# Gate products of a two-layer trunk: branch loads a group ahead, operand splits spread, last token sums in four steps

## The chip, the cores and the metric

The kernel runs on one core of a Trainium2 chip. The metric is the device time of one execution in microseconds (us), as the median of several runs.

## The reference

The model is a trunk of two layers over 1024 latent tokens and 256 context tokens with 1024 channels. In each layer an input projection feeds four token mixers (a, b, cc, d), each of 256 channels, and 4 x 1024 gate columns. The part that matters here is the merge:

```python
def merge_branches(a, b, cc, d, zg, w_a, w_b, w_c, w_d, w_o):
    ga, gb, gc, gd = jnp.split(jax.nn.sigmoid(zg), N_BRANCH, axis=-1)
    m = ga * (a @ w_a) + gb * (b @ w_b) + gc * (cc @ w_c) + gd * (d @ w_d)
    return m @ w_o
```

Here zg is `h @ w_in` for the gate columns, with h the modulated and normed tokens. All data are 32-bit floats. In the last layer only the 1024 latent tokens go through the merge.

## The kernel before

**Precision.** A product of two float arrays is made from three matmuls (`mm3`, L432 to L434). Each operand is split into a high part, rounded on ACT by a copy (L427), and a low part, the difference, on DVE (L428). The matmuls are high by high, high by low, low by high. `split` issues the two instructions of one operand.

**The stage.** `gates_last` (L1210) makes the merge of the last layer. It works through 16 groups: four blocks d of 256 output channels, and for each the four branches i. A group needs the gate (1024 input channels by 256 columns, for 1024 tokens), which goes into two PSUM tiles A of 128x1024, and the branch product (256 channels by 256 columns), which goes into tiles X and T. DVE multiplies the two and adds the product to the sum m.

**Seven products.** Groups 0 and 1 make the gate from four blocks of the weights (x11, x12, x21, x22), 24 matmuls each. From group 2 on, the gate is a 2x2 block matrix product with seven block products instead of eight, of 12 matmuls each. They use sums of weight blocks (s1, s2, s3, s4, made on POOL in `begin`, L1283, and `s4`, L1287) and sums of token blocks (T1 to T4). The list `plan` (L1353) gives the order x11, s2, x12, x22, s3, s1, s4, the quarter q of A that each fills, and its token block. After x11 ACT copies the quarter out (L1360); after s2 DVE makes u2 (L1362); after x12 DVE makes c11 (L1365) and ACT its sigmoid; after s3 c21 (L1368); after s1 three more sums (L1370 to L1372) and a sigmoid (L1373); after s4 the last sum (L1375) and its sigmoid.

**Token sums.** T1, T2 and T3 are made in groups 0 and 1 by the generator `sides` (L1226): four steps, each with three sums on DVE (L1233), three differences on POOL (L1236) and their splits. It is advanced three times after each half product. T4 (L1240 to L1249) takes the room of token block 12 and can only be made after group 1. Group 2 makes all of its four steps at once, by `self.finish(side)` ahead of its first product.

**Order of the work.** Each engine runs its instructions in the order in which the program issues them. The list `ops` holds the splits of the weight operands of all groups in their order of use; `ready(n + 3)` issues them up to two ahead of the product that comes next. The gate weights come through three buffers (`graw`) on the SP queue; a load waits until the last reader of its buffer is done.

**Branches.** `bh_load` (L1323) loads the two halves of the group's branch from DRAM by the POOL queue (L1327), through one buffer `br`, splits each half into bh and bl, and splits the branch weights into wbh and wbl. It is issued after x12 in groups 0 and 1, and after s2 from group 2 on. In the group's last part 24 matmuls form the branch product (tiles X and T, L1390), and DVE multiplies and adds (L1393 to L1396).

Of the kernel before, what the change touches and what calls it, by code (L numbers as in the profile page):

```python
# [8 lines left out]
F32 = mybir.dt.float32  # L9
F32R = mybir.dt.float32r  # L10
BF16 = mybir.dt.bfloat16
I32 = mybir.dt.int32
AF = mybir.ActivationFunctionType
# [404 lines left out]
class Trunk:  # L418
# [791 lines left out]
    def gates_last(self, p, mp):  # L1210
# [9 lines left out]
        Y = {}  # L1220
# [5 lines left out]
        def sides():  # L1226

            for k in range(4):
                t = [mp.tile([128, 1024], F32, name="mr", bufs=2) for _ in range(2)]
                y11, y12, y22 = t[0][:, :512], t[0][:, 512:], t[1][:, :512]  # L1230
                for y, n in ((y11, "11"), (y12, "12"), (y22, "22")):
                    h, lo = Y[n][k]
                    nc.vector.tensor_tensor(y, h.bitcast(F32), lo.bitcast(F32), op=OP.add)  # L1233
                    yield 1
                for o, x, y, n in ((y11, y12, y11, "T1"), (y12, y22, y12, "T3"), (y22, y22, y11, "T2")):
                    nc.gpsimd.tensor_tensor(o, x, y, op=OP.subtract)  # L1236
                    yield 1
                    self.split(*Y[n][k], o)

            while "T4" not in Y:  # L1240
                yield 2
            for k in range(4):
                t = mp.tile([128, 1024], F32, name="mr", bufs=2)
                y21, t2 = t[:, :512], t[:, 512:]
                for y, n in ((y21, "21"), (t2, "T2")):
                    h, lo = Y[n][k]
                    nc.vector.tensor_tensor(y, h.bitcast(F32), lo.bitcast(F32), op=OP.add)
                nc.gpsimd.tensor_tensor(y21, y21, t2, op=OP.subtract)
                self.split(*Y["T4"][k], y21)  # L1249
                yield 3  # L1250

        side = sides()
        ops = []
# [7 lines left out]
        def product(o, w, y, start, stop):  # L1261
            for k in range(4):
                self.mm3(o, w[0][:, k, :], w[1][:, k, :], *Y[y][k], start=start and k == 0, stop=stop and k == 3)
# [3 lines left out]
        def make(gi):  # L1267

            d, i = groups[gi]
            S = {"d": d, "i": i}  # L1270
            G.append(S)

            def x(j, b):
                return S["raw"][j][:, 4 * b:4 * b + 4, :]

            def begin():
                S["raw"] = [st.get()[0] for _ in range(2)]
                S["wb"] = st.get()[0]
                if gi >= 2:
                    s1, s2, s3 = ([p.tile([128, 4, 128], F32, name=n) for n in ("s1", "s2", "s3")])  # L1280
                    for o, a, b, op in ((s1, x(1, 0), x(1, 1), OP.add), (s2, s1, x(0, 0), OP.subtract),
                                        (s3, x(0, 0), x(1, 0), OP.subtract)):
                        nc.gpsimd.tensor_tensor(o, a, b, op=op)  # L1283
                    S["s"] = s1, s2, s3

            def s4():
                nc.gpsimd.tensor_tensor(S["s"][1], x(0, 1), S["s"][1], op=OP.subtract)  # L1287

            if gi < 2:
                names = [("x11", lambda: x(0, 0)), ("x12", lambda: x(0, 1)), ("x21", lambda: x(1, 0)), ("x22", lambda: x(1, 1))]  # L1290
            else:
                names = [("x11", lambda: x(0, 0)), ("s2", lambda: S["s"][1]), ("x12", lambda: x(0, 1)), ("x22", lambda: x(1, 1)),
                         ("s3", lambda: S["s"][2]), ("s1", lambda: S["s"][0]), ("s4", lambda: S["s"][1])]
            for n, f in names:
                def prep(n=n, f=f):
                    if n == "x11":
                        begin()
                    S[n] = operand(f())
                    if n == "s2":
                        S["late"] = True  # L1300
                    if n == "x12" and S.pop("late", None):
                        s4()
                ops.append(prep)
# [5 lines left out]
        def ready(n):  # L1309
            while done[0] < min(n, len(ops)):  # L1310
                ops[done[0]]()
                done[0] += 1
        n = 0
        ready(2)
        add, AC = OP.add, nc.scalar.activation
        halves = [slice(0, 512), slice(512, 1024)]
        for gi, (d, i) in enumerate(groups):
# [2 lines left out]
            q = [A[j // 2][:, halves[j % 2]] for j in range(4)]  # L1320
            g = [p.tile([128, 1024], F32, name="g", bufs=2) for _ in range(2)]

            def bh_load():  # L1323
                S["b"] = []
                for k in range(2):
                    b = p.tile([128, 1024], F32, name="br", bufs=1)
                    nc.gpsimd.dma_start(b, self.br[i][k * 128:(k + 1) * 128, :1024])  # L1327
                    bh, bl = p.tile([128, 1024], F32R, name=f"bh{k}"), p.tile([128, 1024], F32R, name=f"bl{k}")
                    S["b"].append((b, bh, bl))
                    self.split(bh, bl, b)  # L1330
                wh, wl = p.tile([128, 2, 256], F32R, name="wbh"), p.tile([128, 2, 256], F32R, name="wbl")
                self.split(wh, wl, S["wb"])
                S["w"] = wh, wl

            if gi < 2:
                for j, w in enumerate(("x11", "x12", "x21", "x22")):
                    ready(n + 3)
                    for t in range(2):
                        product(q[j // 2 * 2 + t], S[w], "12"[j % 2] + "12"[t], j % 2 == 0, j % 2 == 1)
                        for _ in range(3):  # L1340
                            next(side)
                    n += 1
                    if j == 1:
                        bh_load()
                    if j % 2:
                        AC(g[j // 2], A[j // 2], AF.Sigmoid)
            else:
                if gi == 2:
                    Y["T4"] = Y["12"]
                    self.finish(side)  # L1350
                u2 = p.tile([128, 512], F32, name="u2")
                c11, c12, c21, c22 = g[0][:, :512], g[0][:, 512:], g[1][:, :512], g[1][:, 512:]
                plan = [("x11", 0, "11"), ("s2", 1, "T2"), ("x12", 0, "21"), ("x22", 2, "T4"), ("s3", 1, "T3"),  # L1353
                        ("s1", 3, "T1"), ("s4", 0, "22")]
                for j, (w, o, y) in enumerate(plan):
                    ready(n + 3)
                    product(q[o], S[w], y, True, True)
                    n += 1
                    if w == "x11":
                        AC(c11, q[0], AF.Copy)  # L1360
                    elif w == "s2":
                        nc.vector.tensor_tensor(u2, q[1], c11, op=add)  # L1362
                        bh_load()
                    elif w == "x12":
                        nc.vector.tensor_tensor(c11, q[0], c11, op=add)  # L1365
                        AC(c11, c11, AF.Sigmoid)
                    elif w == "s3":
                        nc.vector.tensor_tensor(c21, q[1], u2, op=add)  # L1368
                    elif w == "s1":
                        nc.vector.tensor_tensor(c22, q[3], c21, op=add)  # L1370
                        nc.vector.tensor_tensor(c12, q[3], u2, op=add)
                        nc.vector.tensor_tensor(c21, q[2], c21, op=add)  # L1372
                        AC(g[1], g[1], AF.Sigmoid)  # L1373
                    elif w == "s4":
                        nc.vector.tensor_tensor(c12, q[0], c12, op=add)  # L1375
                        AC(c12, c12, AF.Sigmoid)
# [3 lines left out]
            if i == 0:  # L1380
                self.mp = m = mp.tile([128, 2, 1024], F32, name="mp")
            wh, wl = S["w"]
            for j in range(2):
                ready(n + 2 + j)
                for t in range(2):
                    s = halves[t]
                    o = self.ps.tile([128, 512], F32, name="XT"[t])
                    for k in range(2):
                        c = slice(128 * j, 128 * j + 128)
                        self.mm3(o, wh[:, k, c], wl[:, k, c], S["b"][k][1][:, s], S["b"][k][2][:, s],  # L1390
                                 start=(k == 0), stop=(k == 1))
                    if i == 0:
                        nc.vector.tensor_tensor(m[:, j, s], o, g[j][:, s], op=OP.mult)  # L1393
                    else:
                        nc.vector.tensor_tensor(g[j][:, s], o, g[j][:, s], op=OP.mult)
                        nc.vector.tensor_tensor(m[:, j, s], m[:, j, s], g[j][:, s], op=add)  # L1396
# [778 lines left out]
```

## Time and profile before

| | |
|---|---|
| median of 3 runs | 3649.33 us (3646.88 to 3649.39) |
| profiled execution: time | 3648.42 us |
| profiled execution: span | 3646.6 us |
| mean granted TensorE clock | 0.964 |
| PE busy | 3376.2 us, 93% |
| DVE busy | 2287.4 us, 63% |
| ACT busy | 1616.0 us, 44% |
| POOL busy | 928.9 us, 25% |

The page of the profile belongs to one execution. PE is TensorE's matmuls, PEld its weight loads, DVE VectorE, ACT ScalarE, POOL GpSimd, SP the engine that issues most DMAs. A busy PE is not PE at its peak: a matmul at a lower granted clock is busy for longer. "Idle before" is the time an engine waited ahead of an instruction, with what ended that wait. L427 is line 427 of the kernel.

### The profile page before, as it was taken

How to read it: one execution, taken by the hardware profiler on the slowest of the kernel's cores; microseconds unless marked ns; L12 is line 12 of the kernel's file. 1: busy time of each engine (PE TensorE's matmuls, PEld its weight loads, DVE VectorE, ACT ScalarE, POOL GpSimd, SP SyncE). 2: the span in 40 equal slices, each digit the busy share in tenths (PEclk: the TensorE clock that was granted, in tenths of full speed). 3: DMA queues.
4: the chain of work that ended last, by engine and by line, in shares of the span. 5: the costliest groups of instructions: out<-in, count | busy, mean ns of one | idle time of the engine just before them, and what ended most of it. 6: DMA issues, size and time to landing. Idle time of an engine off the chain costs nothing. (4 is left out here: it accounts for less than half of the span.)

```text
span 3646.6 us, 47270 instructions
## 1 busy us (share of the span) xinstructions
PE 3376.2 (93%) x18567; PEld 2590.7 (71%) x18567; DVE 2287.4 (63%) x3116; ACT 1616.0 (44%) x2203; POOL 928.9 (25%) x798
## 2 busy tenths in 40 slices
PE   7999999999998899999998999878888896999997
PEld 5996788888875566666665797656666675888885
DVE  5856512223265677777776784654555457999997
ACT  4125411111144566556664423532222254777776
POOL 3105100000025433333221112422122143535430
PEclk9999999999999899999999999989999897999998
DMA  6113233333045788888888313222222368999995
GB/s 207 36 54 98 78 98 99 103 93 107 25 168 199 260 293 288 286 287 288 283 288 283 95 41 98 59 65 80 90 76 78 125 218 306 385 387 378 390 385 199
DMA packets 300177, 672.45 MB, mean 184 GB/s; under 512 B 32991, under 2 KB 138325, under 8 KB 299954
## 3 DMA queue, kind: packets, MB, share of 16 engines
q1 hardware_dynamic: 267410, 554.50, 42.7%
q0 software_dynamic: 32368, 114.85, 10.4%
q8 instruction: 146, 2.39, 0.3%
q14 instruction: 77, 0.63, 0.1%
q10 hardware_dynamic: 176, 0.08, 0.0%
HBM read 610.33 MB, written 54.84 MB: 182 GB/s over the span
## 5 line engine op out<-in xcount | busy, mean ns | idle before, releaser
L428 DVE TENSOR_TENSOR wlo<-wraw,whi 128x1024 fp32r<-128x1024 f32 (+1 forms) x882 | 1023.6, 1205 | 470.1 <-ACT whi L427 465.1
L427 ACT ACTIVATE whi<-wraw 128x1024 fp32r<-128x1024 f32 (+1 forms) x882 | 862.4, 1027 | 292.9 <-PE A L434 264.5
L432 PE MATMUL A<-hTh,whi 128*128 128x512 f32 x1056 | 426.0, 403 | 11.3 <-DVE u L1362 11.0
L432 PE MATMUL A<-whi,xh 128*128 128x512 f32 x1024 | 418.2, 408 | 1.4 <-ACT whi L427 1.4
L434 PE MATMUL A<-hTh,wlo 128*128 128x512 f32 x1056 | 412.9, 391 | 3.6 <-DVE wlo L428 3.6
L433 PE MATMUL A<-hTl,whi 128*128 128x512 f32 x1056 | 412.6, 391 | 3.8 <-POOL hTl L684 2.1
L433 PE MATMUL A<-wlo,xh 128*128 128x512 f32 x1024 | 404.3, 395 | 2.0 <-DVE wlo L428 1.1
L434 PE MATMUL A<-whi,xl 128*128 128x512 f32 x1024 | 402.4, 393 | 0.5 <-DVE xl L428 0.5
L1963 POOL TENSOR_SCALAR oh<-cs,slot 128x128 bf16<-128x128 f32 x232 | 278.2, 1216 | 1.0
L2071 POOL DMA_INDIRECT x<-y,idx x31 | 50.6, 1631 | 843.2 <-DVE y L2070 843.2
L432 PEld LDWEIGHTS A<-hTh,whi 128*128 128x128 f32 x1056 | 199.1, 189 | 67.9 <-DVE u L1362 17.2
L432 PEld LDWEIGHTS A<-whi,xh 128*128 128x128 f32 x1024 | 193.8, 189 | 66.4 <-issue 15.1
L434 PEld LDWEIGHTS A<-hTh,wlo 128*128 128x128 f32 x1056 | 198.4, 188 | 48.3 <-DVE wlo L428 5.7
L433 PEld LDWEIGHTS A<-hTl,whi 128*128 128x128 f32 x1056 | 199.1, 189 | 44.1 <-POOL hTl L684 3.0
L433 PEld LDWEIGHTS A<-wlo,xh 128*128 128x128 f32 x1024 | 194.0, 189 | 45.5 <-DVE wlo L428 10.2
L434 PEld LDWEIGHTS A<-whi,xl 128*128 128x128 f32 x1024 | 193.4, 189 | 43.3 <-DVE xl L428 1.2
L1173 ACT ACTIVATE g<-A 128x1024 f32<-128x1024 f32 x32 | 32.9, 1029 | 398.8 <-PE A L434 325.6
L432 PE MATMUL A<-whi,gh 128*128 128x512 f32 x512 | 208.5, 407 | 0.2 <-ACT gh L427 0.2
L433 PE MATMUL A<-wlo,gh 128*128 128x512 f32 x512 | 202.5, 396 | 0.9 <-DVE wlo L428 0.9
L434 PE MATMUL A<-whi,gl 128*128 128x512 f32 x512 | 201.6, 394 | 0.0
L948 DVE SCALAR_TENSOR_TENSOR cacc<-cy,par,cacc 128x1310 f32<-128x1310 f32 (+1 forms) x120 | 190.9, 1591 | 3.4
L433 PE MATMUL A<-wlo,hTh 128*128 128x256 f32 x592 | 168.8, 285 | 10.1 <-DVE wlo L428 10.1
(469 smaller groups left out, 6542.7 us busy)
## 6 DMA issues: line engine op xcount, KB each, us to landing
wraw<-in_w_up_e_dram SPq DMA_DIRECT2D x126, 1024.0 KB, 6.7
wraw<-in_w_gate_e_dram SPq DMA_DIRECT2D x125, 1024.0 KB, 8.4
wraw<-in_w_down_e_dram SPq DMA_DIRECT2D x122, 1024.0 KB, 7.6
wraw<-in_w_in_dram SPq DMA_DIRECT2D x96, 512.0 KB, 4.2
wraw<-in_w_mod_dram SPq DMA_DIRECT2D x68, 512.0 KB, 4.3
br<-br POOLq DMA_DIRECT2D x32, 512.0 KB, 3.7
wraw<-in_w_mod_dram SPq DMA_DIRECT2D x14, 1024.0 KB, 8.3
h<-h POOLq DMA_DIRECT2D x16, 520.0 KB, 3.2
```

Of the source, the lines that this page charges most:

```text
L427: nc.scalar.activation(hi, src, AF.Copy)
L428: (eng or nc.vector).tensor_tensor(lo, src, hi.bitcast(F32), op=OP.subtract)
L432: mm(out, lh, rh, start=start, stop=False)
L433: mm(out, lh, rl, start=False, stop=False)
L434: mm(out, ll, rh, start=False, stop=stop)
L948: nc.vector.scalar_tensor_tensor(acc[:, j, :], y[:, w:w + n_out], wc, acc[:, j, :], op0=OP.mult, op1=OP.add)
L1173: nc.scalar.activation(g[:, :SEQ], A, AF.Sigmoid)
L1963: eng.tensor_scalar(S["oh"][:, t, :], iota, self.slot[:, t, e:e + 1], None, op0=OP.is_equal)
L2071: nc.gpsimd.indirect_dma_start(out=self.x1[l][:, :], out_offset=bass.IndirectOffsetOnAxis(ap=S["idx"][:, :1], axis=0), in_=y, in_offset=No ...
```

## The change

The branches of a group are loaded a group ahead, on ACT's queue, into two buffers: the first group's ahead of the loop, and each next group's just before the branch products. `bh_load` is cut into three parts, `branch(0)`, `branch(1)` (a half of the branch each) and `branch(2)` (the branch weights). They are issued after x12, x21 and x22 in groups 0 and 1, and after s2, x12 and x22 from group 2 on. The T4 steps of group 2 are issued one ahead of each product, each step's split one step later. Group 2 alone makes x22, which needs T4, as its last product, and the sum and the sigmoid that need it (`sum21`) after it.

```diff
             while "T4" not in Y:
                 yield 2
+            last = None
             for k in range(4):
...
                 nc.gpsimd.tensor_tensor(y21, y21, t2, op=OP.subtract)
-                self.split(*Y["T4"][k], y21)
+                if last:
+                    self.split(*last)
+                last = (*Y["T4"][k], y21)
                 yield 3
+            self.split(*last)
+            yield 3
...
+            if gi == 2:
+
+                names.append(names.pop(3))
             for n, f in names:
...
         n = 0
+        B = {}
+
+        def b_load(gi):
+            i = groups[gi][1]
+            B[gi] = [p.tile([128, 1024], F32, name="br", bufs=2) for _ in range(2)]
+            for k in range(2):
+                nc.scalar.dma_start(B[gi][k], self.br[i][k * 128:(k + 1) * 128, :1024])
         ready(2)
+        b_load(0)
...
-            def bh_load():
-                S["b"] = []
-                for k in range(2):
-                    b = p.tile([128, 1024], F32, name="br", bufs=1)
-                    nc.gpsimd.dma_start(b, self.br[i][k * 128:(k + 1) * 128, :1024])
-                    bh, bl = p.tile([128, 1024], F32R, name=f"bh{k}"), p.tile([128, 1024], F32R, name=f"bl{k}")
-                    S["b"].append((b, bh, bl))
-                    self.split(bh, bl, b)
-                wh, wl = p.tile([128, 2, 256], F32R, name="wbh"), p.tile([128, 2, 256], F32R, name="wbl")
-                self.split(wh, wl, S["wb"])
-                S["w"] = wh, wl
+            S["b"] = []
+
+            def branch(k):
+
+                if k == 2:
+                    wh, wl = p.tile([128, 2, 256], F32R, name="wbh"), p.tile([128, 2, 256], F32R, name="wbl")
+                    self.split(wh, wl, S["wb"])
+                    S["w"] = wh, wl
+                    return
+                bh, bl = p.tile([128, 1024], F32R, name=f"bh{k}"), p.tile([128, 1024], F32R, name=f"bl{k}")
+                self.split(bh, bl, B[gi][k])
+                S["b"].append((None, bh, bl))
 
             if gi < 2:
...
-                    if j == 1:
-                        bh_load()
+                    if j:
+                        branch(j - 1)
                     if j % 2:
                         AC(g[j // 2], A[j // 2], AF.Sigmoid)
             else:
                 if gi == 2:
                     Y["T4"] = Y["12"]
-                    self.finish(side)
...
+                if gi == 2:
+                    plan.append(plan.pop(3))
+
+                def sum21():
+                    nc.vector.tensor_tensor(c21, q[2], c21, op=add)
+                    AC(g[1], g[1], AF.Sigmoid)
                 for j, (w, o, y) in enumerate(plan):
                     ready(n + 3)
+                    if gi == 2:
+                        next(side, None)
                     product(q[o], S[w], y, True, True)
                     n += 1
                     if w == "x11":
                         AC(c11, q[0], AF.Copy)
                     elif w == "s2":
                         nc.vector.tensor_tensor(u2, q[1], c11, op=add)
-                        bh_load()
+                        branch(0)
                     elif w == "x12":
                         nc.vector.tensor_tensor(c11, q[0], c11, op=add)
                         AC(c11, c11, AF.Sigmoid)
+                        branch(1)
+                    elif w == "x22":
+                        branch(2)
+                        if gi == 2:
+                            sum21()
                     elif w == "s3":
                         nc.vector.tensor_tensor(c21, q[1], u2, op=add)
                     elif w == "s1":
                         nc.vector.tensor_tensor(c22, q[3], c21, op=add)
                         nc.vector.tensor_tensor(c12, q[3], u2, op=add)
-                        nc.vector.tensor_tensor(c21, q[2], c21, op=add)
-                        AC(g[1], g[1], AF.Sigmoid)
+                        if gi > 2:
+                            sum21()
...
             wh, wl = S["w"]
+            if gi + 1 < len(groups):
+                b_load(gi + 1)
             for j in range(2):
                 ready(n + 2 + j)
```

## Rows read from the trace of the kernel before

**Rows 1.** Windows: groups 0 and 1, group 2, groups 3 to 15, and their sum.

```profile
core 0: us, PE busy (x) PEld busy (x) DVE busy (x) ACT busy (x) POOL busy (x), PEclk, DMA share, GB/s
2343.69:2409.70 66.01, 57.89 (x241) 45.76 (x241) 40.05 (x51) 22.39 (x33) 25.84 (x21) 0.95 0.26 80
2409.70:2458.82 49.12, 29.43 (x110) 22.79 (x109) 25.26 (x37) 11.60 (x18) 12.07 (x11) 0.79 0.18 54
2458.82:2888.15 429.33, 355.21 (x1407) 278.99 (x1406) 221.36 (x314) 116.91 (x179) 83.44 (x80) 0.92 0.27 84
sum 544.46, PE 442.53 PEld 347.53 DVE 286.68 ACT 150.90 POOL 121.35; mean PE 147.51 PEld 115.84 DVE 95.56 ACT 50.30 POOL 40.45
```

**Rows 2.** Waits of PE in the stage: us in total, times, longest.

```profile
PE A L432 <- DVE g L1365: 58.5, 14, 6.9
PE A L432 <- ACT g L1360: 24.4, 14, 15.4
PE A L432 <- DVE u L1362: 11.0, 14, 0.8
```

**Rows 3.** Timeline of PE, group 3: start us, us, instruction, idle before.

```profile
2458.82 0.39 PE L432 MATMUL A<-hTh,whi 128*128 128x512 f32 x1
...
2462.39 0.50 PE L432 MATMUL A<-T2h,whi 128*128 128x512 f32 x1 [0.69 <-ACT g L1360]
...
2466.19 0.50 PE L432 MATMUL A<-hTh,whi 128*128 128x512 f32 x1 [0.78 <-DVE u L1362]
...
2475.24 0.77 PE L432 MATMUL A<-T3h,whi 128*128 128x512 f32 x1 [3.29 <-DVE g L1365]
...
2479.52 0.39 PE L432 MATMUL A<-T1h,whi 128*128 128x512 f32 x1
...
2490.40 0.39 PE L432 MATMUL A<-hTh,whi 128*128 128x512 f32 x1
```

**Rows 4.** Windows, group 3: x12 and x22, then s3; columns as rows 1.

```profile
2466.20:2471.60 5.40, 5.40 (x24) 4.41 (x24) 1.06 (x1) 0.63 (x1) 0.54 (x1) 1.00 0.38 125
...
2475.20:2479.60 4.40, 4.37 (x13) 3.51 (x14) 1.29 (x2) 2.12 (x4) 2.44 (x2) 0.64 0.15 50
```

**Rows 5.** Timelines of DVE, POOL and ACT, group 3: the chain to L1365.

```profile
2465.44 0.69 DVE L1362 TENSOR_TENSOR u<-A,g 128x512 f32<-128x512 f32 x1 [1.86 <-PE A L434]
...
2467.57 0.54 POOL L1327 DMA_DIRECT2D br<-br  x1 [10.61 <-DMA wraw<-in_w_in_dram]
...
2470.97 1.06 ACT L427 ACTIVATE bh<-br 128x1024 fp32r<-128x1024 f32 x1 [7.17 <-DMA br<-br]
...
2474.41 0.68 DVE L1365 TENSOR_TENSOR g<-A,g 128x512 f32<-128x512 f32 x1
```

**Rows 6.** Groups of instructions by form, in the stage: busy us, mean ns, idle before.

```profile
L427 ACT ACTIVATE bh<-br 128x1024 fp32r<-128x1024 f32 x32 | 33.8, 1056 | 134.1 <-DMA br<-br 134.1
L428 DVE TENSOR_TENSOR bl<-br,bh 128x1024 fp32r<-128x1024 f32 x32 | 39.2, 1225 | 95.5 <-ACT bh L427 95.4
L427 ACT ACTIVATE whi<-s 128x512 fp32r<-128x512 f32 x56 | 33.1, 614 | 0.0
L1373 ACT ACTIVATE g<-g 128x1024 f32<-128x1024 f32 x14 | 14.9, 1061 | 105.6 <-DVE g L1372 105.6
L1283 POOL TENSOR_TENSOR s<-wraw 128x512 f32<-128x512 f32 x28 | 41.3, 1476 | 121.0 <-DVE wlo L428 119.1 <-DMA wraw<-in_w_in_dram 1.9
```

**Rows 7.** From issue to landing in the stage: branch loads (L1327), then weight loads (L135).

```profile
DMA to landing us min/median/max: 3.3/3.7/5.8
...
DMA to landing us min/median/max: 2.7/3.8/6.0
```

**Rows 8.** Timeline of PE, group 2: the first matmul of s2.

```profile
2427.98 0.79 PE L432 MATMUL A<-T2h,whi 128*128 128x512 f32 x1 [15.40 <-ACT g L1360]
```

**Rows 9.** Timelines of PE, POOL and ACT, group 0.

```profile
2372.11 0.79 PE L432 MATMUL X<-bh,wbh 128*128 128x512 f32 x1 [5.37 <-ACT wbh L427]
...
2355.45 4.64 POOL L1236 TENSOR_TENSOR mr<-mr 128x512 f32<-128x512 f32 x3 [3.13 <-DVE mr L1233]
...
2372.07 1.28 ACT L1346 ACT_TABLE_LOAD   x1
```

## The prediction

> **What bounds the kernel now.** I first cut the stage out of the trace by windows [rows 1]: its 16 groups take 544.5 us of the span, 66.0 for groups 0 and 1, 49.1 for group 2 and 429.3 for groups 3 to 15, which is 33.0 each. PE is busy 442.5 of the 544.5, but that busy time includes matmuls at half clock: the granted clock is 0.92 in the last stretch and 0.79 in group 2. So the question is what PE does between and during its waits. The waits of PE [rows 2] name one big one: the third quarter of a group waits for the DVE add of L1365, 58.5 us in 14 waits. Two small ones, on L1360 and L1362, stand beside it.
>
> The matmuls of group 3 in order of time [rows 3] give the price. x11 starts at 2458.82, s2 at 2462.39, x12 at 2466.19, s3 at 2475.24, s1 at 2479.52, and the next group at 2490.40. The last part holds 48 matmuls (s1, s4 and the branch products) in 10.88 us without a break, so one matmul of 128x512 costs 0.2267 us. x12 and x22, 24 matmuls, need 5.44 and are done at 2471.63: s3 then waits 3.6 us, and its 12 matmuls take 4.28 instead of 2.72. That is the clock: the granted clock is 1.00 while x12 and x22 run and 0.64 in s3 [rows 4], so part of s3 runs at 1.2 GHz where the others have 2.4. One wait costs 3.6 + 1.6 = 5.2 us here, and 33.0 - 26.4 = 6.6 on average over the groups, since a late branch transfer lengthens it.
>
> What is L1365 late for? Nothing of its own; x12 was done at 2469. It is queued on DVE behind the second branch's split. The chain [rows 5]: u at 2465.44 on DVE, then the first branch's bl, which frees the one buffer; POOL issues the second load at 2467.57, ACT splits it at 2470.97, then DVE does bl, wbl, the split of s3, and L1365 at 2474.41. s3 starts 0.15 us after that add ends. PE waits for it although s3 writes the other half of the PSUM tile; the same is seen at s2 (for L1360) and x12 (for L1362), so a product waits for all earlier readers of its tile A.
>
> **The change in a steady group (3 to 15).** I set time 0 at x11's first matmul and lay the new order out, with the durations of [rows 6]: 1.06 for bh, 1.23 for bl, 0.61 for a whi or wbh, 1.06 for a sigmoid of 1024 columns; 0.7 for a DVE operation of 512 columns by L1365 [rows 5].
> PE keeps its two small waits: s2 at 3.57, x12 at 7.37, x22 at 10.09, end of x22 at 12.81.
> ACT: copy of c11 until 3.5, whi of x22, then bh0 at once, because both branches were loaded a group ahead, until 5.1, whi of s3 until 5.7. DVE: u at 6.6 to 7.3, bl0 to 8.5, wlo of s3 to 9.1, then L1365, waiting for x12, 10.3 to 11.0. So s3, due at 12.81, finds operand and PSUM tile ready 1.8 us early: the wait goes, and with it the low clock.
> Next on ACT: sigmoid of c11 to 11.65, bh1 to 12.7, whi of s1, wbh, whi of s4 to 14.3. On DVE: bl1 to 14.0, wlo of s1 to 14.6, wbl, wlo of s4 to 15.9. s1 starts at 15.53 and its first low-part weights are wanted 0.45 later: 1.4 us of margin, the least of the group. s4 at 18.25 and the branch products at 20.97 find theirs. What stalls would be late next is thus s1's operand.
> POOL loses 32 issues of 0.54 (first: L1327 in [rows 5]); it was not on the path except through the buffer. It does the next group's sums at 14.6 to 19, before they are wanted at 21.
> The 32 loads go to ACT's queue, after the sigmoid of c12 at 23.9. No row of this stage has an ACT issue; the nearest is POOL's 0.54. I take that, 1.1 a group: ACT has only one whi (0.6) before the next copy of c11 at 29.3, so 4.8 us are free and the cost is nothing. The bounds are 0 and, if ACT were held until the data land, the 5.8 of the slowest landing; that case is a rival below. The loads land 3.3 to 5.8 after issue [rows 7], at 31 at the latest, that is 4.4 in the next group, and bh0 could begin as late as 9 before L1365 passes 12.8. Two buffers are free by then: bl1 ended at 14.
> The group is 3.57 + 3.80 + 5.44 + 2.72 + 10.88 = 26.4 us. 13 groups of 33.0 become 13 of 26.4: **-86**.
>
> **Group 2.** In the kernel before all four T4 steps run before s2: PE waits 15.40 us [rows 8] and starts again at half clock. After the change one step is issued ahead of each of the first four products, the last split ahead of the fifth, and T4's product is last. Laid out in the same way: DVE has two more adds and a split per step, so u is at 6.7, L1365 ends at 11.75, and s3, now straight behind x12 (done at 10.1), waits 1.6; s4 waits 0.6 for L1368. x22 runs from 20.6 to 23.3. A new wait follows. x22's split is now late (to 18.4), and it is the last reader of a weight buffer that the next group's second load waits for. That load takes 3.8 [rows 7]: 22.4. POOL then needs two sums of 1.48 [rows 6], ACT 0.6 for whi of the next s2, and only behind that stands wbh, 26.6. The branch products start 3.3 late, with 1.6 of low clock as in s3: the group ends at 33.8. It was 49.1: **-15**. Bounds: 29 (no wait at all) to 39 (landing at 6.0 and lower clock longer).
>
> **Groups 0 and 1.** Here the change moves a split to the wrong side. wbh was issued after x12; PE still waited 5.37 for it, at 2372.11 [rows 9], because of the one buffer. Now branch(2) is issued after x22, behind the third and fourth steps of the T sums, whose chain is serial: two adds (1.4), 4.64 on POOL [rows 9], split and its DVE half (1.3). The second step's POOL work ends at 2360.1. Behind it ACT now does bh0, the table load of 1.28 [rows 9], a sigmoid, a whi and the split, so DVE ends that step at 2364.3; the third step ends with bh1, a whi and bl1 among it at 2373.3; the fourth reaches its T3 split on ACT at 2378.3, and wbh ends at 2378.9. PE waits 6.9 longer, and about 0.9 more in low clock and for wbl. Groups 0 and 1 lost 66.0 - 240 x 0.2267 = 11.6 in all; 6.2 of that is other small waits, and I take 2.6 of it as gained in group 1, where no T step stands among the branch splits any more. Net **+5**, bounds -5 and +12.
>
> **The sum.** -86 - 15 + 5 = -96. The profiled execution took 3648.4; that gives 3552. The median of the three runs stands 0.9 above it: **3553**. The work behind the stage starts on the last branch product, so the gain should pass to the end whole.
>
> **The rivals.**
> *The clock swings all the same.* Two short waits remain in every group (0.69 and 0.78, [rows 3]). If the clock fell after them as it does after s3's wait, each group would give 1.6 back, 13 x 1.6 = 21: 3574. Against it: after both of them x12 and x22 run at 1.00 [rows 4].
> The Trainium skill, page "TensorE: Matmul & The Clock Gate", section "A second HAM failure mode: psum-queue depth-cycling", holds that frequent micro-idles between groups of matmuls are enough to make the clock swing. By that rule this rival would be the likely case; the trace of this kernel does not agree at these two waits.
> *s1 waits in s3's place.* Its operand stands behind bh1 and bl1 with 1.4 us to spare. If DVE and ACT run 3.4 late (sums on POOL slow DVE, a branch lands late), PE waits 2 us a group, 26 in all: 3579.
> *The loads come no earlier.* If the loads on ACT were held until the group they belong to, L1365 would stay late in groups 3 to 15 and only -15 + 5 would remain: 3643. For it: nothing but that ACT is in order; against it, both buffers are free 10 us before.
> *Slower: ACT held by its loads.* If an issue on ACT holds the engine for h until its data land, the next copy of c11, and so s2, is late by 2h - 4.8, and 1.6 of low clock follows. At 3.7 [rows 7] that is 4.2 a group, 55 in all: 3608. It decides against the change from h = 5.3 on, where 13 x 7.4 eats the 96; at 5.8 it is 13 x 8.4 = 109: 3662. Against it: POOL's issues took 0.54 whatever the landing.
>
> **How the numbers follow.** Forecast 0.75, s1 waits 0.08, clock 0.07, loads no earlier 0.03, ACT held 0.04, and 0.03 for something in the code around (other buffer addresses at the start of the stage) that I cannot see. The forecast's own bounds are 3553 - 15 (groups 0 to 2 at their good ends) and, with s1 or the clock, 3579; a little beyond gives 3538 to 3582. A measurement of this kernel can tell some 0.2% from no change, 7 us. "Loads no earlier" lies inside that and counts as same, with a part of the unseen; half of "ACT held" is slower. Faster 0.93; same 0.04; slower 0.03.
>
> **What would show it.** Right: no PE wait on L1365 worth naming in groups 3 to 15, s3 at clock 1.00, groups 26 to 27 us long, ACT idle before bh gone, group 0's wait on wbh longer than 5.4 (about 12), and a wait of 3 to 4 ahead of group 2's branch products. Wrong: groups of 28 or more with a wait ahead of s1 or s2, an ACT issue of microseconds, or a granted clock below 1.00 in groups that have only the two small waits.

## The result and the profile after

The changed kernel takes 3552.78 us (median of 6 runs, 3550.01 to 3554.93) against 3649.95 us (6 runs, 3646.88 to 3654.79): a ratio of 0.9732, 95% interval 0.9719 to 0.9744. The forecast was 3553.

The windows of the same three stretches, in the profile of the changed kernel, answer to [rows 1]:

```profile
2340.31:2410.95 70.64, 57.67 (x241) 46.48 (x241) 39.93 (x51) 22.17 (x33) 23.97 (x17) 0.90 0.27 88
2410.95:2445.65 34.70, 27.83 (x109) 20.77 (x108) 26.07 (x38) 11.51 (x18) 11.56 (x8) 0.95 0.22 68
2445.65:2791.32 345.67, 326.53 (x1408) 261.68 (x1407) 234.57 (x313) 116.55 (x179) 75.40 (x55) 1.00 0.32 102
```

Groups 0 and 1 are 4.6 us longer, group 2 is 14.4 shorter, groups 3 to 15 are 83.7 shorter: together the stage loses 93.4 of its 544.5. The granted clock of the last stretch rose from 0.92 to 1.00. The waits of PE in the stage answer to [rows 2]:

```profile
PE X L432 <- ACT wbh L427: 14.4, 2, 11.8
PE A L432 <- DVE u L1386: 11.3, 14, 1.2
PE A L432 <- ACT g L1384: 9.6, 14, 0.7
...
PE A L432 <- DVE g L1389: 1.7, 1, 1.7
```

L1389 is the c11 add, L1365 before: its 58.5 us in 14 waits are one wait of 1.7, in group 2. The two small waits per group are unchanged (L1384 and L1386, before L1360 and L1362), except that L1384 lost the 15.4 us of group 2. The largest are now two waits for wbh: that of group 0, 5.37 before [rows 9] and 11.8 now, and a new one in group 2. The matmuls of group 3 in order of time, for [rows 3]:

```profile
2445.65 0.39 PE L432 MATMUL A<-hTh,whi 128*128 128x512 f32 x1
...
2449.22 0.50 PE L432 MATMUL A<-T2h,whi 128*128 128x512 f32 x1 [0.69 <-ACT g L1384]
...
2453.03 0.50 PE L432 MATMUL A<-hTh,whi 128*128 128x512 f32 x1 [0.79 <-DVE u L1386]
...
2458.64 0.39 PE L432 MATMUL A<-T3h,whi 128*128 128x512 f32 x1
...
2472.24 0.39 PE L432 MATMUL A<-hTh,whi 128*128 128x512 f32 x1
```

s3 starts without a wait, and the group takes 26.6 us. DVE and ACT of the same group show why, against [rows 5]:

```profile
2452.28 0.69 DVE L1386 TENSOR_TENSOR u<-A,g 128x512 f32<-128x512 f32 x1 [1.87 <-PE A L434]
2452.89 1.22 DVE L428 TENSOR_TENSOR bl<-br,bh 128x1024 fp32r<-128x1024 f32 x1
2454.02 0.69 DVE L428 TENSOR_TENSOR wlo<-s,whi 128x512 fp32r<-128x512 f32 x1
2456.12 0.69 DVE L1389 TENSOR_TENSOR g<-A,g 128x512 f32<-128x512 f32 x1 [1.42 <-PE A L434]
2458.46 1.23 DVE L428 TENSOR_TENSOR bl<-br,bh 128x1024 fp32r<-128x1024 f32 x1 [1.65 <-ACT bh L427]
...
2469.32 0.63 ACT L1405 ACTIVATE g<-g 128x512 f32<-128x512 f32 x1 [1.36 <-DVE g L1404]
2469.33 0.81 ACTq L1328 DMA_DIRECT2D br<-br  x2
2470.24 0.63 ACT L427 ACTIVATE whi<-wraw 128x512 fp32r<-128x512 f32 x1 [0.29 <-ACT g L1405]
```

The add now waits for PE, not PE for the add: it starts 10.5 us into the group (the forecast said 10.3) and ends 1.8 ahead of s3. The second half's split comes behind it. The two loads of the next group take 0.81 us of ACT's queue. They are issued while the sigmoid ahead of them still runs, so ACT itself is idle for only 0.29 us before its next copy.

### The profile page after: what moved, and what is told of

Read it like the earlier page. It is cut to its first block, busy times and chain, and to the rows that moved or that the text cites. A ratio compares the mean times of both kernels' runs of the same rounds, so it can differ in the third digit from the quotient of the medians.

```text
span 3548.2 us, 47246 instructions
## 1 busy us (share of the span) xinstructions
PE 3340.8 (94%) x18567; PEld 2570.2 (72%) x18567; DVE 2300.6 (65%) x3116; ACT 1614.9 (46%) x2203; POOL 921.2 (26%) x766
## 3 DMA queue, kind: packets, MB, share of 16 engines
q1 hardware_dynamic: 267410, 554.50, 43.9%
## 4 chain that ended last, share of the span: by engine, by line
PE 49%; issue 7%; DVE 7%; DMA 3%; ACT 3%; POOL 1%; SPq 0%; POOLq 0%; ACTq 0%; DVEq 0%
PE A L432 13%; PE A L433 13%; PE A L434 12%; PE X L1983 4%; DVE wlo L428 2%; DMA x<-y,idx 1%; PE T L2086 1%; ACT whi L427 1%; DVE cacc L948 1%; PE T L2039 1%; DVE y L2101 1%; PE X L434 0%; PE X L433 0%; PE X L432 0%; POOL oh L1994 0%
```

## The experiments

Each variant starts from the changed kernel. The table gives the time of the stage from the profile of each, cut as in [rows 1], since code outside it is the same. The ratio is to the kernel before, measured beside it.

| kernel | groups 0, 1 | group 2 | groups 3 to 15 | stage | median | ratio, 95% interval |
|---|---|---|---|---|---|---|
| before | 66.0 | 49.1 | 429.3 | 544.5 | 3649.95 | |
| changed | 70.6 | 34.7 | 345.7 | 451.0 | 3552.78 | 0.9732 (0.9719 to 0.9744) |
| POOL's queue | 71.2 | 34.9 | 345.6 | 451.7 | 3558.33 | 0.9749 (0.9732 to 0.9765) |
| one buffer, splits spread | 79.1 | 43.9 | 359.6 | 482.7 | 3587.81 | 0.9833 (0.9816 to 0.9849) |
| loads ahead, splits together | 55.5 | 33.4 | 345.7 | 434.6 | 3537.60 | 0.9692 (0.9676 to 0.9708) |
| T4 steps at once | 71.0 | 39.2 | 345.6 | 455.8 | 3560.46 | 0.9752 (0.9736 to 0.9769) |
| other quarters | 71.0 | 33.5 | 318.5 | 422.9 | 3525.01 | 0.9656 (0.9637 to 0.9674) |
| branch splits early | 55.5 | 32.6 | 345.7 | 433.9 | 3534.82 | 0.9680 (0.9658 to 0.9702) |
| early, other quarters | 55.5 | 31.7 | 318.5 | 405.7 | 3507.93 | 0.9605 (0.9589 to 0.9621) |
| sixteen issues | 81.4 | 39.0 | 391.8 | 512.1 | 3615.05 | 0.9900 (0.9883 to 0.9916) |

**Does the queue matter?**

```diff
-                nc.scalar.dma_start(B[gi][k], self.br[i][k * 128:(k + 1) * 128, :1024])
+                nc.gpsimd.dma_start(B[gi][k], self.br[i][k * 128:(k + 1) * 128, :1024])
```

> The changed kernel with its 32 branch loads on POOL's queue again, still a group ahead and into two buffers. Theory (the gain is the removed wait of s3; which queue issues the loads does not matter): 3553, within 0.2%; groups 3 to 15 stay at 26.6 us each, POOL gets 32 issues of about 0.54 us back and no PE wait changes. Rival (the queue is part of the gain, because POOL's loads stand behind its stores and sums): the groups after a store (each fourth) lose several us again, in all 10 to 30 us.

The steady groups are the same within a few hundredths, but the median was 5.5 us above that of the changed kernel, measured on another occasion. So both were run again, side by side.

> The changed kernel as it is, beside its variant with the loads on POOL's queue, on the same chip. The variant's first run gave 3558.3 with the same 26.6 us groups; its excess over 3552.8 lay outside the stage. Theory (which queue issues the loads does not matter, the excess was the chip or the executions): the two ratios come out within 0.1% of each other. Rival (POOL's issues cost something outside the stage's PE row): the variant is 4 to 6 us longer here too.

> The loads on POOL's queue again, for the comparison with the changed kernel on the same chip. Theory: equal within 4 us. Rival: longer by 4 to 6 us, outside the groups 3 to 15.

The changed kernel gave 3553.12 (ratio 0.9725, 0.9712 to 0.9738), the variant 3554.76 (0.9732, 0.9719 to 0.9746), in 5 runs each, and the stage 451.7 and 450.2 in their profiles. The queue does not matter to the time within this noise: the medians are 1.6 us apart. The medians from issue to landing do differ; the two lines are POOL's in the first of its runs, then ACT's in the changed kernel:

```profile
DMA to landing us min/median/max: 3.7/4.5/6.5
```

```profile
DMA to landing us min/median/max: 3.4/3.7/5.8
```

The 0.8 us are not like for like. The loads go out in pairs, and the trace has a landing for all 32 of POOL's loads but for only 20 of ACT's. The first of a pair lands after 3.85 us on POOL and 3.48 on ACT (medians), the second after 4.55 and 4.59. Either way the data are there long before the next group wants them. The Trainium skill says in "DMA: Bandwidth & Descriptors", section "Issuing engines are not separate DMA queues", that issuing from another engine only saves the issuing engine's time. These runs agree: an issue takes 0.4 us on ACT or 0.55 on POOL, and the stage takes the same.

**Loading ahead, or spreading the splits?** First without the loads ahead:

```diff
-                self.split(bh, bl, B[gi][k])
+                b = p.tile([128, 1024], F32, name="br", bufs=1)
+                nc.gpsimd.dma_start(b, self.br[i][k * 128:(k + 1) * 128, :1024])
+                self.split(bh, bl, b)
...
-        b_load(0)
...
-            if gi + 1 < len(groups):
-                b_load(gi + 1)
```

> The changed kernel without the loads ahead: one buffer, each half loaded on POOL's queue where it is split, as in the kernel before; the splits stay spread. Theory A (the wait went because nothing late stands ahead of the c11 add on DVE; the spread alone does that): s3 does not wait. The second load is issued when bl0 is done (8.5 us into the group), lands at 12.2 (at 14.3 for the slowest landing), and s1's low part is then ready at 15.2 to 17.3 against 16.0 wanted: groups of 26.6 to 28, in all 3553 to 3575. Rival B (loading ahead is what removes the wait): s3, or s1 in its place, waits 3 us or more with low clock behind it, groups of 31 to 33, in all 3610 to 3640.

Neither holds throughout. Ten of the 13 steady groups take 26.5 to 27.0 us, as theory A has it. Groups 4, 8 and 12 take 30.3, 31.7 and 30.9, group 0 takes 51.9 and group 2 43.9: 31.7 us more in the stage. POOL's timeline at the start of group 4 (2487.74) shows what those three have in common:

```profile
2488.24 0.56 POOL L1429 DMA_DIRECT2D mD<-mp  x1 [2.17 <-DVE mp L1426]
2491.50 0.55 POOL L1429 DMA_DIRECT2D mD<-mp  x1 [2.70 <-DVE mp L1426]
2492.04 0.53 POOL L1349 DMA_DIRECT2D br<-br  x1
2500.01 0.53 POOL L1349 DMA_DIRECT2D br<-br  x1 [7.43 <-DVE bl L428]
```

The group's first load stands behind the two stores of the block before it, 4.3 us into the group; in the other steady groups it is issued before the group starts. The wait is then ahead of s1, whose operand stands behind the late second half on ACT:

```profile
2505.48 0.50 PE L432 MATMUL A<-T1h,whi 128*128 128x512 f32 x1 [1.41 <-ACT whi L427]
```

The same three are the longest steady groups of the kernel before, with 36.3, 35.1 and 36.3 us. In group 0 PE waits 21.2 us for wbh. There a load stands behind POOL's three token differences, and ACT's split behind the load:

```profile
2364.92 4.55 POOL L1236 TENSOR_TENSOR mr<-mr 128x512 f32<-128x512 f32 x3 [9.88 <-DVE mr L1233]
2369.42 0.56 POOL L1349 DMA_DIRECT2D br<-br  x1
...
2373.37 1.06 ACT L427 ACTIVATE bh<-br 128x1024 fp32r<-128x1024 f32 x1 [4.90 <-DMA br<-br]
```

In group 2 PE waits 6.7 us for the c11 add. So the place on POOL's queue costs something where nothing is loaded ahead; how much of groups 0 and 2 it explains was not tested apart.

Then with the loads ahead, but the splits where they were:

```diff
-                    if j:
-                        branch(j - 1)
+                    if j == 1:
+                        for k in range(3):
+                            branch(k)
...
-                        branch(0)
+                        for k in range(3):
+                            branch(k)
...
-                        branch(1)
...
-                        branch(2)
```

> The changed kernel with the loads ahead, but all three splits issued together at their old places (after x12 in groups 0 and 1, after s2 later). Theory A (either part alone removes the steady wait): bl0, bl1, wbl and s3's split follow each other on DVE without a wait, the c11 add ends at 11.8 us of the group, s3 is due at 12.8: groups 3 to 15 stay at 26.6. Group 0 no longer waits 11.8 us for wbh behind the token sums, and group 2 no longer 2.6 behind the next group's operand: 16 to 20 us less with their low clock, 3533 to 3537. Rival B (the spread is needed): s3 waits 1 us or more in every group, 3565 or more.

Theory A. The steady groups stay at 26.6, so there the spread is worth nothing once the loads come early. DVE's timeline in group 3 (start 2434.64) has no gap where the load used to be:

```profile
2441.26 0.69 DVE L1387 TENSOR_TENSOR u<-A,g 128x512 f32<-128x512 f32 x1 [1.86 <-PE A L434]
2441.87 2.35 DVE L428 TENSOR_TENSOR bl<-br,bh 128x1024 fp32r<-128x1024 f32 x2
2444.14 0.68 DVE L428 TENSOR_TENSOR wbl<-wraw,wbh 128x512 fp32r<-128x512 f32 x1
2444.74 0.69 DVE L428 TENSOR_TENSOR wlo<-s,whi 128x512 fp32r<-128x512 f32 x1
2445.34 0.69 DVE L1391 TENSOR_TENSOR g<-A,g 128x512 f32<-128x512 f32 x1
```

The add ends 11.4 us into the group, s3 is due at 13.0. Groups 0 and 1 fall from 70.6 to 55.5: the spread was a loss there. The time is 0.6 us over the range of theory A; in group 2 s3 still waits 3.4 us for the c11 add. Either part alone removes most of the steady loss; the loads ahead remove all of it.

**What are the four T4 steps worth?**

```diff
-            if gi == 2:
-
-                names.append(names.pop(3))
...
                     Y["T4"] = Y["12"]
+                    self.finish(side)
...
-                if gi == 2:
-                    plan.append(plan.pop(3))
...
-                    if gi == 2:
-                        next(side, None)
...
-                        if gi == 2:
-                            sum21()
...
-                        if gi > 2:
-                            sum21()
+                        sum21()
```

> The changed kernel with the four T4 steps of group 2 made at once ahead of its first product, and x22 in its old place. Theory (the steps are worth the 15.4 us wait less what group 2 now waits elsewhere): group 2 goes from 34.7 to about 44 us (49.1 before, less the 5 us of s3's wait), the rest is unchanged, in all 3562. Rival (with the loads ahead, DVE and ACT have room enough that the order of the T4 steps costs nothing): 3553.

Group 2 takes 39.2 against 34.7, half of the difference expected. PE's wait ahead of s2 is back, but it is 11.76 us and no longer 15.40 [rows 8]:

```profile
2432.46 0.79 PE L432 MATMUL A<-T2h,whi 128*128 128x512 f32 x1 [11.76 <-ACT g L1378]
```

The variant does not bring the old steps back whole: each split still comes one step later, so the sums of the second step start on DVE while POOL makes the first difference. Against the 11.76 stand the waits that the spread steps brought: 1.7 ahead of s3 and 2.6 ahead of the branch products. The median, 3560.5, lies between the theories' 3562 and 3553; the profile's 4.5 us in group 2 decides for the first, with a smaller size. What the later splits are worth by themselves was not measured.

**The wait for wbh in groups 0 and 2.**

```diff
-                    if j:
-                        branch(j - 1)
+                    if j == 1:
+                        for k in range(3):
+                            branch(k)
...
                     elif w == "x22":
-                        branch(2)
                         if gi == 2:
                             sum21()
+                        else:
+                            branch(2)
                     elif w == "s3":
+                        if gi == 2:
+                            branch(2)
```

> The changed kernel with all three branch splits after x12 in groups 0 and 1 as before the change, and in group 2 the split of the branch weights after s3 in place of after x22; loads ahead and spread splits stay in groups 3 to 15. Theory (the 11.8 us wait of group 0 is the order of issue behind the token sums, the 2.6 of group 2 the order behind the next group's operand): both go, groups 0 and 1 take 55.6 us as with the splits together, group 2 about 30.5, the rest 345.7, the stage 432, in all 3532 to 3536. Rival (the data, not the order, is late: the branch or its weights): the waits stay, 3553.

The waits are order, not data. In the changed kernel PE waits 11.82 us in group 0, behind the T sums' last split on ACT:

```profile
2375.18 0.79 PE L432 MATMUL X<-bh,wbh 128*128 128x512 f32 x1 [11.82 <-ACT wbh L427]
```

```profile
2371.05 4.58 POOL L1236 TENSOR_TENSOR mr<-mr 128x512 f32<-128x512 f32 x3 [4.26 <-DVE mr L1233]
...
2373.98 0.63 ACT L427 ACTIVATE T3h<-mr 128x512 fp32r<-128x512 f32 x1 [0.71 <-POOL mr L1236]
...
2374.52 0.61 ACT L427 ACTIVATE wbh<-wraw 128x512 fp32r<-128x512 f32 x1
```

In group 2 of the changed kernel wbh stands behind the next group's s2 operand, which waits for a POOL sum:

```profile
2436.76 0.63 ACT L427 ACTIVATE whi<-s 128x512 fp32r<-128x512 f32 x1 [2.63 <-POOL s L1288]
2437.30 0.61 ACT L427 ACTIVATE wbh<-wraw 128x512 fp32r<-128x512 f32 x1
```

With the split early, both waits for wbh are gone. Group 2 falls to 32.6 rather than 30.5, because one product now waits 1.9 us for its own high part on ACT.

**Whose are the two small waits?**

```diff
-                plan = [("x11", 0, "11"), ("s2", 1, "T2"), ("x12", 0, "21"), ("x22", 2, "T4"), ("s3", 1, "T3"),
-                        ("s1", 3, "T1"), ("s4", 0, "22")]
+                plan = [("x11", 0, "11"), ("s2", 2, "T2"), ("x12", 1, "21"), ("x22", 3, "T4"), ("s3", 0, "T3"),
+                        ("s1", 2, "T1"), ("s4", 1, "22")]
```

The sums that read the quarters read the new ones.

> The changed kernel with other quarters of the two PSUM tiles: the seven products go to quarters 0, 2, 1, 3, 0, 2, 1 in place of 0, 1, 0, 2, 1, 3, 0, so that s2 and x12 no longer write the tile that is just being read. Theory (the two small waits come from the tile being shared, not from the quarter): both go, 0.85 and 1.08 us a group with the refill, groups 3 to 15 fall from 26.6 to 24.6 to 24.7, the stage by 25 to 27, in all 3526 to 3530, and the granted clock stays 1.00. Rival (the product waits for the engine's last operation whatever the tile): groups stay at 26.6, in all 3553.

The theory, to the end: in groups 3 to 15 no wait of PE is left, and PE is busy for the whole window.

```profile
2443.63:2762.14 318.51, 318.51 (x1407) 263.67 (x1406) 234.72 (x313) 116.51 (x179) 75.40 (x55) 1.00 0.35 111
```

A group is 24.5 us, which is its 108 matmuls at 0.2267. What made s2 and x12 wait is the shared tile. Group 2 pays for it in part: its wait for the c11 add grows from 1.70 to 4.15.

```profile
2422.65 0.76 PE L432 MATMUL A<-T3h,whi 128*128 128x512 f32 x1 [4.15 <-DVE g L1389]
```

**Both together.** The last two edits in one kernel.

> Both edits of the last two together. If the theories hold, the gains add: 3553 - 19 - 26 = 3508, 3503 to 3513, with groups 3 to 15 at 24.6. If the shorter groups bring another wait forward (s1's operand, DVE's work per group), groups stay above 25.5 and the sum is 3520 or more.

3507.93, ratio 0.9605: better than either edit alone, and the gains add (27.8 and 18.0 us alone, 44.9 together). The steady groups are again 24.5; group 2 keeps one wait of 4.2 for the c11 add, as with the other quarters alone.

**What does an issue hold?**

```diff
-                nc.scalar.dma_start(B[gi][k], self.br[i][k * 128:(k + 1) * 128, :1024])
+                for r in range(0, 128, 16):
+                    nc.scalar.dma_start(B[gi][k][r:r + 16, :], self.br[i][k * 128 + r:k * 128 + r + 16, :1024])
```

> The changed kernel with each branch load cut into eight loads of 16 partitions, so that ACT issues 16 a group in place of 2. The two took 0.81 us together. Theory (an issue holds ACT's queue for some 0.4 us and nothing else; some 4.3 us are free before the next copy of c11): 16 take 6.4 us, 5.6 more, so the copy comes 1.3 or more late and the groups grow from 26.6 to some 28, in all 3570 to 3580. Rival 1 (issuing does not hold the engine's own work): 3553. Rival 2 (ACT is held until the data land): 3600 or more.

Issuing holds ACT's own work, which excludes rival 1. The groups grow to 30.1 on average, more than the 28 expected. ACT and PE between two groups:

```profile
2518.43 7.38 ACTq L1329 DMA_DIRECT2D br<-br  x16
2525.91 0.63 ACT L427 ACTIVATE whi<-wraw 128x512 fp32r<-128x512 f32 x1 [6.85 <-DMA br<-br]
2526.45 0.58 ACT L1385 ACTIVATE g<-A 128x512 f32<-128x512 f32 x1
```

```profile
2495.89 0.79 PE L432 MATMUL A<-T2h,whi 128*128 128x512 f32 x1 [4.40 <-ACT g L1385]
...
2527.08 0.50 PE L432 MATMUL A<-T2h,whi 128*128 128x512 f32 x1 [2.86 <-ACT g L1385]
```

The 16 issues take 7.4 us here, 0.46 each, not 6.4. Ahead of the longest wait of s2, 4.40, they take 8.9, with one issue of 1.14; what held that one is not shown. The copy is late, s2 waits 39.0 us in the 13 groups, and the clock of the stretch falls to 0.95, which my 28 left out. Rival 2 had 3600 or more, and the time, 3615, lies there, but its mechanism does not: `whi` starts 0.1 us after the last issue, and these loads need 2.0 us or more to land. The 6.85 us put down to a DMA in that row are the time of the issues themselves, less the part beside the sigmoid that still ran.

## Why the prediction was right, step by step

| term | forecast | measured in the profile |
|---|---|---|
| groups 3 to 15 | -86, 26.4 each | -83.7, 26.6 each |
| group 2 | -15, 33.8 long | -14.4, 34.7 long |
| groups 0 and 1 | +5, of it a wait of some 12 | +4.6, a wait of 11.82 |
| sum | -96 | -93.4 |

**The steady group.** That L1365 was late only through DVE's order, and s3 only through L1365, is shown: with the add ahead of the second split, or with that split no longer waiting for a load, s3 does not wait. The low clock behind the wait left with it. The term was 2 us too large: I gave x12 and x22 24 matmuls at the pace of an unbroken row, 5.44, and they take 5.61 (2453.03 to 2458.64), because the first few after a wait are slower (0.34 us from the first to the second, then 0.23 to 0.24). 13 x 0.17 is 2.2.

**Groups 0 and 1.** The added wait behind the T sums came as laid out, with low clock behind it (0.90 over the two groups, 0.95 before), and group 1 lost its small waits: 27.2 us, which is 120 x 0.2267. I had 2.6 for that; it was 29.9 - 27.2 = 2.7.

**Group 2.** Both waits that I put there are seen: 1.7 for L1389 (1.6) and 2.55 for wbh (3.3). The 0.6 that I put ahead of s4 is 0.2. The group is 0.9 longer than laid out: the branch products start at 27.0 us, 0.4 later, and then wait another 0.46 for wbl, the low part of the branch weights, which the sum left out.

**The cost of an ACT issue.** 0.4 in place of the 0.54 taken from POOL; without an effect on PE, as forecast. The sixteen issues bound the room there was: 7.4 us a group are too much, 0.81 are not.

**The rivals.** The clock does not swing at the two small waits: 1.00 over groups 3 to 15, with both waits in every group. What the Trainium skill reports of another kernel in "TensorE: Matmul & The Clock Gate", section "A second HAM failure mode: psum-queue depth-cycling", that frequent micro-idles between groups of matmuls made the clock oscillate, is not borne out here, with waits of 0.7 and 0.8. s1 does not wait, the loads do come earlier, and ACT is not held until the data land. One sum among the rivals is wrong: 3649.3 - 15 + 5 is 3639 for loads that come no earlier, not 3643. That is 10 us from no change and not inside the 7 that the text allows, so the 0.03 of that rival belongs to faster; the forecast does not rest on it.

**What was luck.** The stage gave 93.4, the span 98.4 (3646.6 to 3548.2): the stage began 3.4 us earlier in this execution, and the rest was 1.6 shorter. Over the twelve profiles of this study the stage begins between 2338.1 and 2351.1, with the same code ahead of it. So the agreement of 3553 with 3552.8 is closer than the terms can claim; they are good to some 3 us.

## What to carry to other kernels

A late load costs at the first in-order engine that has other work behind it: here a split on DVE waited for a branch that nobody needed yet, and the sum that PE did need stood behind it. Load a stage ahead, and then look where the splits stand: the same move that adds nothing in the steady groups once the loads come early cost 15 us in group 0 (43.4 against 28.3), where it put a short operand behind a long serial chain. When a product waits for a reader of another part of its own PSUM tile, let consecutive products alternate between tiles; that was worth 27 us of 451 here and needed only other indices.

## What was not expected of the hardware

Of two loads of 512 KB issued one behind the other, the second landed 0.7 us later after its issue than the first on POOL (4.55 against 3.85) and 1.1 later on ACT (4.59 against 3.48). An ACT issue held the queue for 0.4 us when two stood together and 0.46 in a row of sixteen. It ran beside the activation that had started just before it, and held up only what came behind: two issues of 0.81 left ACT idle for 0.29. After a wait of 0.7 to 0.8 us the next 24 matmuls took 0.17 us more than an unbroken row, with the granted clock at 1.00 throughout.
